# Opening stage of a two-layer diffusion trunk: squares added on the vector engine, modulation rows of five parts made between the products, three tile pairs begun instead of four

## The chip, the cores and the metric

The kernel runs as one program on one core of a Trainium2 chip. The metric is the device time of one execution in microseconds (us), as the median of repeated runs. All times inside an execution below are counted from the start of the profiled span.

## The reference

A trunk of two layers works on 256 latent tokens of 1024 features and on 256 context tokens that pass through the first layer only. Every layer is a half-step SwiGLU, a token mixer (attention with pooling in layer 0, a gated spatial unit in layer 1), and a second half-step SwiGLU. Each of the three begins with an RMS norm and a modulation whose shift, scale and gate are a product of the conditioning vector and a large matrix:

```python
def rms_norm(x, g):
    xf = x.astype(jnp.float32)
    y = xf * lax.rsqrt(jnp.mean(xf * xf, axis=-1, keepdims=True) + EPS)
    return (y * g.astype(jnp.float32)).astype(x.dtype)

def modulate(x, g, shift, scale):
    return rms_norm(x, g) * (1 + scale) + shift

def swiglu(h, w13, w2):
    a, b = jnp.split(h @ w13, 2, axis=-1)
    return (jax.nn.silu(a) * b) @ w2

# in each layer, first sub-layer:
m = (silu(c) @ w_mod[i] + b_mod[i]).reshape(b, 1, 9, d)     # the context has its own, from c_ctx
x = x + 0.5 * m[:, :, 2] * swiglu(modulate(x, norm_g[i, 0], m[:, :, 0], m[:, :, 1]), w13, w2)
```

Everything is float32. Features are 1024 = 8 parts of 128, the inner width of a SwiGLU is 2816 = 22 parts of 128.

## The kernel before

Activations lie with features on the 128 partitions, so an activation is 8 parts (index `k`) of 128 x 512: columns 0 to 255 are the latent tokens (`st` 0), 256 to 511 the context tokens (`st` 1). `X` holds the stream, `rb` the reciprocal norms of all tokens, repeated on every partition.

A float32 product is made as three products in the faster format fp32r (`mm3`): a matrix is split into a high part, which ScalarE rounds (`S.copy`, a CAST in the profile), and a low part, the remainder, which VectorE subtracts. `AH` and `AL` are the two parts of the normed activation, `sh`, `sl`, `whi` and `wlo` those of weights. One tile pair `f` of the first SwiGLU (128 columns of `a` and the 128 of `b` that belong to them) takes, for each part `k`, two groups of three products of 128 x 512.

The modulation is made in two ways. `use_mod` lets VectorE multiply 128 rows of the transposed matrix (a tile `wm`, 512 KB) with the repeated conditioning vector `cc` and sum along the row; it is needed for shift and scale of a part and for both token kinds, so four of these instructions per part. `by_rows` lets TensorE multiply the conditioning vectors (128 x 2 as the stationary operand) with natural columns of the matrix, which gives a row that is then turned to partitions by further small products. `finish_mod` adds the bias and makes `gs`, the norm's gain times (1 + scale). The two vectors `gs` and `mod` of a part are needed before its activation can be normed.

`start` is the opening stage, in which nothing can be multiplied before the norms and the first modulation are there. It

- loads the conditioning vectors, `ident`, the first `wm`, and `X` in four transfers of 512 KB, and repeats the conditioning vectors with 16 products (L630), copied by ScalarE into `cc`;
- squares the parts of `X` on ScalarE (L644), lets TensorE sum each over the partitions and over the parts in one accumulation (L645), and takes root (L646) and reciprocal (L650) of all 512 columns;
- makes the modulation of part 0 with `use_mod` and that of parts 5, 6 and 7 together in one `by_rows` (L662, L666, L669) ahead of all products;
- then goes over the parts in the order 0, 5, 1, 6, 2, 7, 3, 4, and for each makes the split of four tile pairs' weights, the normed activation, and the products of four tile pairs into 8 PSUM banks that stay open over all parts. The modulation of parts 1 to 4 is made by `use_mod` on the way.

`ffn` takes the four begun pairs over and goes on with pair 4. While it runs, `run_mods` makes the rest of the modulation at a set rate per pair.

A scheduler that records the instructions decides their order on each engine; instructions that pass through `keep_in_program_order` (`pin`) hold their order among themselves. Transfers of weights and `X` are all issued by SyncE's queue (SP), those of `run_mods` by GpSimd's (POOL). Tiles of one name share a ring of `bufs` buffers, and a transfer into a buffer waits for the last reader of it.

## Time and profile before

| | |
|---|---|
| median of 3 runs | 1154.62 us (1152.18 to 1155.01) |
| the profiled execution | 1152.68 us, its span 1150.9 us, granted TensorE clock 0.999 |
| TensorE (PE) busy | 1132.6 us, 98% of the span |
| VectorE (DVE) busy | 874.2 us, 76% |
| ScalarE (ACT) busy | 521.6 us, 45% |
| first product of the opening's tile pairs | 28.38 us |
| end of the fourth pair's last product (its Silu begins) | 73.74 us |

PE is the engine of the products, PEld its loads of stationary operands, which run beside them. A row of the timeline has the start, the duration, the engine, the line of the code, the operation, the tile written and those read, the shape, how many such instructions follow each other, and in brackets how long the engine had been idle and what ended that. A float32 product that isn't split has two records, one that is fp32r has one. Since instructions overlap in an engine's pipeline, the distance from start to start is what an instruction takes in a row of others, and the duration is how long its result takes.

### The profile page before, as it was taken

How to read it: one execution, taken by the hardware profiler on the slowest of the kernel's cores; microseconds unless marked ns; L12 is line 12 of the kernel's file. 1: busy time of each engine (PE TensorE's matmuls, PEld its weight loads, DVE VectorE, ACT ScalarE, POOL GpSimd, SP SyncE). 2: the span in 40 equal slices, each digit the busy share in tenths (PEclk: the TensorE clock that was granted, in tenths of full speed). 3: DMA queues.
4: the chain of work that ended last, by engine and by line, in shares of the span. 5: the costliest groups of instructions: out<-in, count | busy, mean ns of one | idle time of the engine just before them, and what ended most of it. 6: DMA issues, size and time to landing. Idle time of an engine off the chain costs nothing.

```text
span 1150.9 us, 19103 instructions
## 1 busy us (share of the span) xinstructions
PE 1132.6 (98%) x7646; PEld 1031.1 (90%) x7646; DVE 874.2 (76%) x1614; ACT 521.6 (45%) x814; POOL 68.4 (6%) x140
## 2 busy tenths in 40 slices
PE   8999999999999997899999999999999999999998
PEld 4878888888888895699999999999999899999998
DVE  5967787878789989778778788656767688756663
ACT  5552212222223456565334456434445866534442
POOL 0000110122222100000010000000000000000000
PEclk9999999999999999999999999999999999999999
DMA  8844656788888840556587656446546536546543
GB/s 318 309 147 156 194 185 232 275 299 317 303 289 303 318 159 10 183 183 219 180 312 261 229 193 219 162 155 225 184 142 247 185 132 210 182 152 226 179 146 116
DMA packets 52408, 242.72 MB, mean 211 GB/s; under 512 B 5600, under 2 KB 11488, under 8 KB 38880
## 3 DMA queue, kind: packets, MB, share of 16 engines
q1 hardware_dynamic: 33888, 174.39, 42.8%
q0 software_dynamic: 18432, 67.12, 17.5%
q8 instruction: 60, 0.98, 0.3%
q14 instruction: 28, 0.23, 0.1%
HBM read 240.44 MB, written 1.05 MB: 210 GB/s over the span
## 4 chain that ended last, share of the span: by engine, by line
PE 93%; DVE 4%; ACT 1%; DMA 1%; issue 1%; SPq 0%; ACTq 0%; DVEq 0%
PE ps L148 29%; PE ps L149 29%; PE ps L150 29%; PE ps L662 1%; PE ps L583 1%; PE ps L584 1%; PE ps L582 1%; PE ps L645 1%; DMA raw<-in_w 1%; PE ps L630 1%; DVE st L445 1%; DVE wlo L154 1%; DVE wm L80 1%; DVE junk L80 0%; PE ps L472 0%
## 5 line engine op out<-in xcount | busy, mean ns | idle before, releaser
L148 PE MATMUL ps<-AH,wlo 128*128 128x258 f32 (+2 forms) x1664 | 507.9, 306 | 0.3 <-ACT AH L153 0.3
L149 PE MATMUL ps<-AH,whi 128*128 128x258 f32 (+2 forms) x1664 | 507.2, 305 | 0.0
L150 PE MATMUL ps<-AL,whi 128*128 128x258 f32 (+2 forms) x1664 | 506.1, 305 | 0.0
L153 ACT CAST whi<-raw 128x1024 fp32r<-128x1024 f32 (+2 forms) x354 | 313.6, 921 | 364.5 <-PE ps L150 254.6
L154 DVE TENSOR_TENSOR wlo<-raw,whi 128x1024 fp32r<-128x1024 f32 (+2 forms) x354 | 367.7, 1065 | 53.6 <-ACT whi L153 52.8
L148 PEld LDWEIGHTS ps<-AH,wlo 128*128 128x128 f32 x1664 | 317.1, 191 | 16.3 <-issue 1.0
L149 PEld LDWEIGHTS ps<-AH,whi 128*128 128x128 f32 x1664 | 315.0, 189 | 14.7 <-issue 0.5
L150 PEld LDWEIGHTS ps<-AL,whi 128*128 128x128 f32 x1664 | 314.1, 189 | 14.2 <-DVE AL L154 0.2
L150 PE MATMUL ps<-HL,whi 128*128 128x256 f32 (+1 forms) x704 | 218.0, 310 | 0.0
L149 PE MATMUL ps<-HH,whi 128*128 128x256 f32 (+1 forms) x704 | 218.0, 310 | 0.0
L148 PE MATMUL ps<-HH,wlo 128*128 128x256 f32 (+1 forms) x704 | 218.0, 310 | 0.0
L80 DVE CUSTOM_DVE_ANT_0 wm<-wm,cc 128x1024 f32<-128x1024 f32 x138 | 165.0, 1221 | 6.1 <-DMA wm<-in_w_mod 5.4
L150 PEld LDWEIGHTS ps<-HL,whi 128*128 128x128 f32 x704 | 132.5, 188 | 7.8
L149 PEld LDWEIGHTS ps<-HH,whi 128*128 128x128 f32 x704 | 132.6, 188 | 7.7
L148 PEld LDWEIGHTS ps<-HH,wlo 128*128 128x128 f32 x704 | 132.5, 188 | 7.7
L72 POOL DMA_DIRECT2D wm<-in_w_mod x128 | 67.7, 529 | 553.8 <-DVE mod L80 507.0
L206 ACT ACTIVATE sa<-sa,cb 128x256 f32<-128x256 f32 x66 | 33.6, 510 | 120.4 <-DVE sa L205 117.0
L246 DVE SCALAR_TENSOR_TENSOR X<-ps,gate,X 128x256 f32<-128x256 f32 x64 | 30.9, 483 | 47.4 <-PE ps L150 47.2
L204 DVE COPY cb<-ps 128x1 f32<-128x1 f32 x66 | 10.3, 156 | 73.6 <-PE ps L150 73.5
L80 DVE CUSTOM_DVE_ANT_0 junk<-wm,cc 128x1024 bf16<-128x1024 f32 x34 | 41.5, 1219 | 8.8 <-ACT cc L632 8.1
L212 DVE TENSOR_TENSOR h<-ps,sa 128x512 f32<-128x512 f32 x22 | 15.2, 693 | 42.1 <-PE ps L150 33.6
L154 DVE TENSOR_TENSOR HL<-h,HH 128x256 fp32r<-128x256 f32 (+1 forms) x88 | 42.4, 485 | 0.0
(160 smaller groups left out, 709.5 us busy)
## 6 DMA issues: line engine op xcount, KB each, us to landing
raw<-in_w SPq DMA_DIRECT2D x84, 1024.0 KB, 4.9
wm<-in_w_mod POOLq DMA_DIRECT2D x128, 512.0 KB, 5.0
raw<-in_w SPq DMA_DIRECT2D x64, 704.0 KB, 4.1
wm<-in_w_mod SPq DMA_DIRECT2D x10, 512.0 KB, 6.9
raw<-in_w_in_a SPq DMA_DIRECT2D x5, 1024.0 KB, 8.5
raw<-in_w SPq DMA_DIRECT2D x8, 512.0 KB, 6.2
raw<-in_w_out_a SPq DMA_DIRECT2D x4, 1024.0 KB, 4.8
raw<-in_w_in_cu SPq DMA_DIRECT2D x4, 1024.0 KB, 4.9
```

Of the source, the lines that this page charges most:

```text
L72: eng.dma_start(out=w, in_=I["w_mod"][layer, i])
L80: pin(V.tensor_tensor_reduce(out=res, in0=w, in1=cc[:, st, :], scale=1.0, scalar=0.0, op0=ALU.mult, op1=ALU.add, accum_out=mod[:, 2 * laye ...
L148: PE.matmul(ps, wl, xh, start=first, stop=False)
L149: PE.matmul(ps, wh, xh, start=False, stop=False)
L150: PE.matmul(ps, wh, xl, start=False, stop=last)
L153: S.copy(hi, src)
L154: pin(V.tensor_tensor(out=lo, in0=src, in1=hi.bitcast(F32), op=ALU.subtract))
L206: S.activation(out=sa[:, :T], in_=sa[:, :T], func=AF.Silu, bias=cb[:, 0:1])
L212: V.tensor_tensor(out=h32[:, :n], in0=ps[1][:, :n], in1=sa[:, :n], op=ALU.mult)
L246: V.scalar_tensor_tensor(out=X[:, m, :T], in0=ps[:, :T], scalar=gate[:, 2 * layer, sub, m:m + 1], in1=X[:, m, :T], op0=ALU.mult, op1=ALU.add)
L445: V.reduce_max(out=st[:, 0:1], in_=ps[g], axis=AX.X)
L582: PE.matmul(ps[b], AL[:, k, ts], hi[:, ws], start=(k == 0), stop=False)
```

## The change

Only the opening stage is different, with the packing of its inputs.

- ScalarE squares the parts, VectorE adds them up in `acc`, and TensorE sums over the partitions once, in two halves of 256 columns. Root and reciprocal are taken in halves, too.
- `X` comes in eight transfers ahead of all weights.
- Parts 3 to 7 get their modulation from `by_rows`, one part at a time: 1 MB of natural columns, eight products of 32 columns (the vectors and zeros) by 256, put on four column groups of TensorE's array (`rw[32 * g:32 * g + 32]`) in two rounds, a copy on ScalarE, and two small products with a 0/1 matrix `sel` that add the four groups and turn the row. For each but the first part this stands between the products of the part ahead of it. Parts 0, 1 and 2 get theirs from `use_mod`.
- The order of the parts is 3, 4, 0, 5, 1, 6, 2, 7. The first part's products go in halves of 256 columns, high parts first.
- Three tile pairs are begun; the fourth is made by `ffn` like the rest.

The diff without the packing and the details of the split:

```diff
     def start():
-        ng = 4
-        order = (0, 5, 1, 6, 2, 7, 3, 4)
+        ng = 3
+        order = (3, 4, 0, 5, 1, 6, 2, 7)
+
+        jobs = {1: 0, 2: 1, 4: 2}
...
-            wm = {(0, 0): load_mod(0, 0, nc.sync)}
-            for k in range(0, NK, 2):
-                nc.sync.dma_start(out=X[:, k:k + 2], in_=I["xc"][:, k:k + 2])
-            wm[0, 1] = load_mod(0, 1, nc.sync)
...
+            for k in range(NK):
+                nc.sync.dma_start(out=X[:, k], in_=I["xc"][:, k])
+            nc.sync.dma_start(out=par, in_=I["par"])
+            rows, raws, wm = {}, {}, {}
+            rows[3] = get_rows(3)
+            raws[3] = get_raw(3)
+            rows[4] = get_rows(4)
+            raws[4] = get_raw(4)
+            wm.update({(0, j): load_mod(0, j, nc.sync) for j in range(2)})
+            raws[0] = get_raw(0)
...
             for k in range(NK):
-                sq = tmp.tile([P, 2 * T], F32, name="sq", bufs=2)
-                S.activation(out=sq, in_=X[:, k], func=AF.Square)
-                PE.matmul(ps, ones, sq, start=k == 0, stop=k == NK - 1)
-            S.activation(out=rb, in_=ps, func=AF.Sqrt, scale=1.0 / D, bias=epsb)
-            for h in range(2):
-                use_mod(0, h, wm[0, h])
-            finish_mod(0, 0, 2, slice(0, 1))
-            V.reciprocal(rb, rb)
+                square_acc(k, 2 * T)
+            ps = bank()
+            for st in range(2):
+                ts = slice(st * T, st * T + T)
+                PE.matmul(ps[:, ts], ones, acc[:, ts], start=True, stop=True)
+                S.activation(out=rb[:, ts], in_=ps[:, ts], func=AF.Sqrt, scale=1.0 / D, bias=epsb)
+            rw = bank()
+            pin(V.reciprocal(rb[:, :T], rb[:, :T]))
+
+            def by_rows(k):
+                w = rows.pop(k)
+                for kt in range(NK):
+                    g = kt % 4
+                    pin(PE.matmul(rw[32 * g:32 * g + 32, :2 * P], c32[:, kt], w[:, kt],
+                                  start=kt < 4, stop=kt >= 4))
+                row = sp.tile([P, 2 * P], F32, name="row", bufs=2)
+                pin(S.copy(row, rw[:, :2 * P]))
+                for j in range(2):
+                    PE.matmul(rw[:, 2 * P + 2 * j:2 * P + 2 * j + 2], row[:, j * P:j * P + P], sel,
+                              start=True, stop=True)
+                finish_mod(0, 0, 2, slice(k, k + 1),
+                           rw[:, 2 * P:2 * P + 4].rearrange("p (j s) -> p s j", j=2).unsqueeze(3))
...
+                if i in jobs:
+                    d = jobs[i]
                     for j in range(2):
-                        use_mod(0, 2 * nxt + j, wm.get((nxt, j)) or
-                                load_mod(0, 2 * nxt + j, nc.sync), tc.keep_in_program_order)
+                        use_mod(0, 2 * d + j, wm.pop((d, j)), tc.keep_in_program_order)
+                    finish_mod(0, 0, 2, slice(d, d + 1))
...
+                ahead = order[i + 1] if i + 1 < NK and order[i + 1] in ROWS else None
+                if i == 0:
+                    for ts in halves:
+                        if ts.start:
+                            by_rows(ahead)
+                        for j, (a, x) in enumerate(((0, AH), (0, AL), (1, AH))):
+                            for f, ab in ws:
+
+                                PE.matmul(pss[f][ab][:, ts], ws[f, ab][a], x[:, k, ts],
+                                          start=j == 0 and ts.start == 0, stop=False)
+                else:
+                    for f, ab in ws:
+                        if ahead is not None and (f, ab) == (1, 0):
+                            by_rows(ahead)
+                        mm3(pss[f][ab], *ws[f, ab], AH[:, k, :2 * T], AL[:, k, :2 * T], False,
+                            i == NK - 1)
```

What that does to the order of instructions is shown at three places. The first is VectorE's start, from the first modulation to the first normed part; in the kernel before it reads (L80 is `use_mod` and the read of its sum, L92 and L98 are `finish_mod`, L686 is the activation times `rb`):

```order
L80 ISA junk,mod<-wm,cc 128x1024
L80 ISA mod 128x1
L80 ISA wm,mod<-wm,cc 128x1024
L80 ISA mod 128x1
L80 ISA junk,mod<-wm,cc 128x1024
L80 ISA mod 128x1
L80 ISA wm,mod<-wm,cc 128x1024
L80 ISA mod 128x1
L92 TENSOR_TENSOR mod<-mod,par 128x2x2
L98 SCALAR_TENSOR_TENSOR gs<-mod,par 128x2
L650 RECIPROCAL rb<-rb 128x512
L686 TENSOR_TENSOR sa<-X,rb 128x512 x3
```

The same place on VectorE in the changed kernel (L93 and L100 are `finish_mod`, here of part 3; L714 and L726 the activation times `rb`, L696 the low parts of the weights, L704 the activation's):

```order
L638 MEMSET c_111 128x256
L165 TENSOR_TENSOR acc<-acc,sq 128x512 x7
L660 RECIPROCAL rb<-rb 128x256
L93 TENSOR_TENSOR mod<-ps,par 128x2x2
L100 SCALAR_TENSOR_TENSOR gs<-mod,par 128x2
L714 TENSOR_TENSOR sa<-X,rb 128x256
L711 RECIPROCAL rb<-rb 128x256
L696 TENSOR_TENSOR sl<-raw_99,sh 128x512
L696 TENSOR_TENSOR wlo<-raw_99,whi 128x256
L704 TENSOR_TENSOR AL<-h_190,AH 128x256
L714 TENSOR_TENSOR sa<-X,rb 128x256
L726 TENSOR_TENSOR sa<-X,rb 128x512
```

The four modulation instructions of part 0 are gone from this place, and seven additions stand there. The second place is where they went: VectorE behind the low part of part 4's activation (`h_259`); `raw_109` holds the weights of part 0, `raw_271` those of part 5.

```order
L156 TENSOR_TENSOR AL<-h_259,AH 128x512
L81 ISA junk,mod<-wm,cc 128x1024
L81 ISA mod 128x1
L696 TENSOR_TENSOR wlo<-raw_109,whi 128x256
L81 ISA wm,mod<-wm,cc 128x1024
L81 ISA mod 128x1
L81 ISA junk,mod<-wm,cc 128x1024
L81 ISA mod 128x1
L696 TENSOR_TENSOR sl<-raw_271,sh 128x512
L81 ISA wm,mod<-wm,cc 128x1024
L81 ISA mod 128x1
L696 TENSOR_TENSOR wlo<-raw_271,whi 128x256
```

The two instructions of `finish_mod` for part 0 follow it directly. The third place is TensorE from the sums of squares to the first products; before:

```order
L645 MATMUL ps<-sq,ones 128x512 x8
L662 MATMUL ps<-raw,cT 2x384 x8
L662 MATMUL ps<-whi,cT 2x384 x4
L662 MATMUL ps<-wlo,cT 2x384 x4
L669 MATMUL ps<-ident,row 128x2 x3
L148 MATMUL ps<-AH,sl 128x512
L149 MATMUL ps<-AH,sh 128x512
L150 MATMUL ps<-AL,sh 128x512
L669 MATMUL ps<-ident,row 128x2 x3
L148 MATMUL ps<-AH,sl 128x512
```

and in the changed kernel (L655 the sums, L668 and L673 a `by_rows`, first of part 3, then of part 4; L760 the products of part 3):

```order
L655 MATMUL ps<-acc,ones 128x256 x2
L668 MATMUL ps<-raw,c_111 32x256 x8
L673 MATMUL ps<-cs,row 128x2 x2
L760 MATMUL ps<-AH,sh 128x256 x4
L760 MATMUL ps<-AH,whi 128x256 x2
L760 MATMUL ps<-AL,sh 128x256 x4
L760 MATMUL ps<-AL,whi 128x256 x2
L760 MATMUL ps<-AH,sl 128x256 x4
L760 MATMUL ps<-AH,wlo 128x256 x2
L668 MATMUL ps<-raw,c_111 32x256 x8
L760 MATMUL ps<-AH,sh 128x256 x4
L673 MATMUL ps<-cs,row 128x2 x2
```

The 24 products of squares and rows ahead of the first tile pair became ten shorter ones, and the rows of the other parts stand between the products.

More of the change, by code (lines that the diff above doesn't have):

```diff
@@ L625, in start @@
-            for st in range(2):
-                for h in range(2):
-                    ps = bank()
-                    for k4 in range(4):
-                        k = 4 * h + k4
-                        PE.matmul(ps[:, k4 * P:k4 * P + P], cT[:, st, k:k + 1].broadcast_to([P, P]),
-                                  ident, start=True, stop=True)
-                    S.copy(cc[:, st, h * 512:h * 512 + 512], ps)
-            nc.sync.dma_start(out=par, in_=I["par"])
-            wn = [wpool.tile([P, 2, 2 * NR * P], F32, name=n, bufs=3 if i > 1 else 2)
-                  for i, n in enumerate(("raw", "raw", "whi", "wlo"))]
@@ L697, in start @@
[L697 to L707 removed]
+                parts = ((sh[:, k], sl[:, k], raw[:, :2]), (wh[:, k], wl[:, k], raw[:, 2]))
```

141 lines of the change are left out of this document (82 added, 59 removed).

## The prediction

> **What bounds the kernel now.** I read the page's busy times and its chain first, then the waits of PE, then windows over the opening, then the timeline there.
>
> ```profile
> PE 1132.6 (98%) x7646; PEld 1031.1 (90%) x7646; DVE 874.2 (76%) x1614; ACT 521.6 (45%) x814; POOL 68.4 (6%) x140
> PE 93%; DVE 4%; ACT 1%; DMA 1%; issue 1%; SPq 0%; ACTq 0%; DVEq 0%
> ```
>
> ```profile
> PE ps L463 <- DVE sa L451: 6.5, 5, 1.9
> PE ps L630 <- DMA ident<-in_ident: 3.3, 1, 3.3
> ...
> PE ps L148 <- ACT AH L153: 0.3, 1, 0.3
> ```
>
> TensorE bounds the kernel: once products run they wait 0.3 us in the opening and else only in the mixer (L463), which the change doesn't touch. So only the moment counts at which a given amount of tile-pair work is done. In the windows (PE, PEld, DVE, ACT busy) and PE's timeline of the opening:
>
> ```profile
> 0.00:28.38 28.38, 25.11 (x87) 12.37 (x87) 15.12 (x24) 14.79 (x26) 0.20 (x4) 1.00 0.85 317
> 28.38:75.00 46.62, 46.56 (x203) 37.35 (x203) 39.38 (x81) 26.93 (x52) 2.24 (x4) 1.00 0.68 239
> 40.00:50.00 10.00, 10.00 (x45) 8.12 (x44) 10.00 (x23) 7.38 (x15) 0.66 (x1) 1.00 0.96 336
> ```
>
> ```profile
> 3.27 6.76 PE L630 MATMUL ps<-ident,cT 128*128 128x128 f32 x32 [3.27 <-DMA ident<-in_ident]
> 9.86 7.42 PE L645 MATMUL ps<-sq,ones 128*128 128x512 f32 x16
> 17.21 5.32 PE L662 MATMUL ps<-raw,cT 128*2 128x384 f32 x16
> 22.37 2.74 PE L662 MATMUL ps<-whi,cT 128*2 128x384 f32 x8
> 24.95 2.74 PE L662 MATMUL ps<-wlo,cT 128*2 128x384 f32 x8
> 28.38 0.50 PE L148 MATMUL ps<-AH,sl 128*128 128x512 f32 x1
> ...
> 44.00 0.39 PE L148 MATMUL ps<-AH,wlo 128*128 128x512 f32 x1
> 49.56 0.40 PE L148 MATMUL ps<-AH,wlo 128*128 128x512 f32 x1
> ```
>
> ```profile
> 73.74 0.60 ACT L211 ACTIVATE sa<-ps 128x512 f32<-128x512 f32 x1 [0.27 <-PE ps L150]
> ```
>
> PE's first 28 us go to repeating (L630), squares (L645) and rows (L662). Then it is dense: 24 products from 44.00 to 49.56, 0.232 each. VectorE is full beside it (10.00 of 10) but isn't waited for: a part of the activation has 24 products, 5.6 us, and that covers what VectorE does for a later part. The 192 products of the four pairs are done at 73.7 (the Silu of pair 3 waits for the last). That is the mark: when does the changed kernel have the same four pairs (three begun, one in `ffn`)?
>
> **The change part by part.** Durations in a row, start to start, on VectorE:
>
> ```profile
> 37.76 1.22 DVE L80 CUSTOM_DVE_ANT_0 wm<-wm,cc 128x1024 f32<-128x1024 f32 x1
> ...
> 38.91 1.23 DVE L80 CUSTOM_DVE_ANT_0 junk<-wm,cc 128x1024 bf16<-128x1024 f32 x1
> ...
> 40.05 0.69 DVE L154 TENSOR_TENSOR sl<-raw,sh 128x512 fp32r<-128x512 f32 x1
> 40.66 1.22 DVE L80 CUSTOM_DVE_ANT_0 wm<-wm,cc 128x1024 f32<-128x1024 f32 x1
> ...
> 41.80 0.42 DVE L154 TENSOR_TENSOR wlo<-raw,whi 128x256 fp32r<-128x256 f32 x1
> 42.14 0.16 DVE L92 TENSOR_TENSOR mod<-mod,par 128x4 f32<-128x4 f32 x1
> ```
>
> A modulation instruction costs 1.15, a 512-wide operation 0.60, a 256-wide one 0.34. On ScalarE and for the norm:
>
> ```profile
> 2.58 1.28 ACT L623 ACT_TABLE_LOAD   x1
> 7.50 1.15 ACT L644 ACTIVATE sq<-X 128x512 f32<-128x512 f32 x2 [1.56 <-DMA X<-in_xc]
> 8.55 1.05 ACT L632 COPY cc<-ps 128x512 f32<-128x512 f32 x2
> 17.32 0.69 ACT L646 ACTIVATE rb<-ps,epsb 128x512 f32<-128x512 f32 x1 [1.22 <-PE ps L645]
> 22.15 1.09 ACT L689 ACTIVATE h<-sa,mod,gs 128x256 f32<-128x256 f32 x2 [4.15 <-DVE sa L686]
> 23.28 0.62 ACT L153 CAST AH<-h 128x512 fp32r<-128x512 f32 x1
> 27.09 0.47 ACT L666 COPY row<-ps 2x384 f32<-2x384 f32 x1 [2.06 <-PE ps L662]
> ```
>
> ```profile
> 18.04 3.35 DVE L650 RECIPROCAL rb<-rb 128x512 f32<-128x512 f32 x1 [2.53 <-ACT rb L646]
> ```
>
> ```profile
> 5.00:10.00 5.00, 5.00 (x27) 5.00 (x27) 0.85 (x1) 2.69 (x5) 0.00 (x0) 1.00 1.02 398
> ```
>
> *Squares.* `X`'s first pair landed at 7.50 with 1.12 MB moved; now its last part is at 2.17 MB, so 7.5 + 1.05 / 0.40 = 10.1, its first at 5.6. ScalarE then does a square (0.53), a table load (1.28) and root (0.3), seven squares and four copies (0.5 each), so the last square ends at 13.0, not the transfer but ScalarE last. Addition 0.69, half a sum on PE 0.6, half a root 0.46: VectorE begins the reciprocal at 15.0 instead of 18.04.
>
> *Rows.* 256 columns by L662's pace (384 columns: 5.32 - 0.49 over 15 steps, 0.32) would be 0.215 a record, two records a product. With output on two halves of the array the trace has:
>
> ```profile
> 453.24 0.63 PE L463 MATMUL ps<-ident,h 128*128 128x128 f32 x4 [0.23 <-DVE h L451]
> 453.80 1.95 PE L472 MATMUL ps<-pt,VV 128*64 128x256 f32 x16
> 455.68 0.70 PE L425 MATMUL ps<-pd,poolw 128*128 128x256 f32 x2
> ```
>
> ```profile
> 520.00:540.00 20.00, 20.00 (x168) 20.00 (x167) 16.27 (x32) 10.65 (x15) 0.53 (x1) 1.00 0.68 237
> ```
>
> At L472 the step is (1.95 - 0.38) / 15 = 0.105, half of 0.215, so halves overlap. Four groups are bounded by 0.054 (a quarter) and 0.215 (no overlap); I take 0.065, near the quarter: 16 records 1.0 us a part, plus two turning products 0.5. A block in the middle of products costs PE 1.5, and up to 0.4 more for entering and leaving (0.31 lie between the last L472 start and 455.68, against 0.105 in a row).
>
> *First part.* Rows of part 3 lie beside the reciprocal. Reciprocal half 1.7, `mod` and `gs` 0.7 with the wait for the turn, multiplication 0.4, norm on ScalarE 0.6: first product at 18.6, 9.8 earlier than 28.38. That is the whole gain. It needs no transfer later than part 3's rows (3.3 MB, 13.0).
>
> *What comes late next.* VectorE goes on in order: second reciprocal 1.7, low parts 0.6 + 0.34, `AL` 0.4, and PE's second and third group of six and the rows of part 4 (1.0), copy (0.4), turn (0.6) follow it: `gs` of part 4 at 25.1. Meanwhile PE waits 1.6 for the first `AL` and ends part 3 at 26.4. Behind `gs`, ScalarE norms part 4 (1.1), casts a weight that stands ahead (0.5) and then `AH` (0.6): part 4 starts at 27.6, after 1.2 of waiting, and ends at 31.8.
>
> From 25.1 VectorE has hardly a gap, and its order (second place shown above) puts four modulation instructions ahead of each of the next two parts that PE needs. To `gs` of part 0: five 512-wide operations (3.0), three 256-wide (1.0), four L80 (4.6), small ones (0.5), so 34.4. ScalarE norms (1.1), casts a weight (0.5) and `AH` (0.6), with hand-overs of some 0.05: PE starts part 0 at 36.9, a wait of 5.1.
>
> To `gs` of part 5: VectorE waits 1.2 until the norm of part 0 frees a buffer of `sa`; then four 512-wide (2.4), two 256-wide (0.7), four L80 (4.6), small ones (0.5): 43.9. ScalarE does three half norms (1.6) and the cast (0.6): PE starts part 5 at 46.3. Part 0, with its block of rows, took PE until 43.0, a wait of 3.3.
>
> So a part now has 18 products, 4.2 us, where VectorE needs 4.6 us for its L80 alone. Part 0's four lay between 9 and 15 us, where VectorE was free (15.12 of 28.38); now they stand in its full stretch, and what PE won by starting early it waits away at parts 0 and 5.
>
> *The rest.* After 46.3 PE has five parts of 18 and pair 3's 48 products, 138 x 0.232 = 32.0, two more rows blocks (3.1), about 1.0 before part 6 (its turn leaves nine products, 2.1, to cover `gs`, norm and cast, 3.0), and 0.2 of small hand-overs: 82.6. Before: 73.7. Sum +8.9. Check on PE alone: 18.6 + 192 products 44.5 + four blocks 6.2 + waits 13.3 = 82.6.
>
> *Edits at nothing.* The seven additions (4.2) lie in VectorE's free time beside ScalarE's squares; without that cover they would cost their 4.2. The fourth pair's move into `ffn` is the same products. Its weights wait on SP for the buffer of part 6's rows, which PE reads near 52; 1 MB at 0.40 takes 2.6 and lands by 58, its first use is after 67. Part 3's halves are two products of 256 for one of 512: the window just quoted, in a stage with 256 latent tokens, has 168 records in 20 us, 0.12 each, so 0.3 in all. On SP the rows of part 5 wait for PE to have read part 3's (16), with part 5's weights and part 1's `wm` behind them; these land between 23 and 27 and are used from 28 on. If a transfer came late there, its lateness would add to a wait of part 0 that is there anyhow. `run_mods` gets one more turn, beside 11 us of products. POOL's queue starts as before.
>
> Against the profiled execution 1152.68 + 8.9 = 1161.6. It lies 1.9 under the median 1154.62, so by the median 1163.5; I put 1162.5, between the two. About 0.3%, 3.5 us, is what a measurement here can tell from no change.
>
> **The rivals.**
>
> *A, TensorE runs at half pace in the gaps' wake.* L630's 32 records of 128 x 128 take 6.76, 0.21 each, while L463's four of the same shape are begun within 0.56 (453.24 to 453.80), 0.14 each. The slow ones follow 3.27 us of idleness, though the granted clock reads 1.00 in both. Now PE idles from 10.0 to 13.8 and for 5 us before part 0; the trace of before has no wait over 1.9 once PE has begun. If all PE work from the sums to part 4 went at half pace, the half sum (+0.4), two blocks of rows with their turns (+3.0) and the groups of six ahead of part 4's rows (+2.2) would lie on the path: 5.6 to 5.8, so 1168. Were part 0 alone slow, its 4.2 would grow into the wait of part 5 and push part 5's rows by 2: 1164.5. The Trainium skill, "TensorE: Matmul & The Clock Gate", Part 1, "What's actually happening", says the array's clock falls to half after an idle window of about 3.4 us and rises after a busy one of that length. By that rule the gap at 10.0 is just long enough and the sum would be 1168 instead of 1162.5; the trace agrees for the start (0.21 against 0.14) and has no such gap to show the rest. Chance 0.22.
>
> *B, the column groups don't overlap.* A block of rows takes 16 x 0.215 = 3.4 instead of 1.0. On top of the forecast the first two lie on the path to `gs` of part 4 (+4.8), part 5's fills a wait, and parts 6's and 7's stand between products (+5): 1172. For it speaks that no row shows four groups, against it L472 with two. Chance 0.07.
>
> *C, the change gains: PE sets the pace.* Were VectorE's stretch from `gs` of part 4 to `gs` of part 5 not waited for, PE would be done at 18.6 + 44.5 + 6.2 = 69.3, 4.4 us earlier than 73.7: 1149. It decides where `gs` of part 5 comes before 35.0 (43.9 less 8.9). VectorE's rows in that stretch add to 18 us without a wait, so even a start 3 us earlier isn't enough. Chance 0.07.
>
> *D, no change to tell.* The gap is half closed if the path to `gs` of part 4 is VectorE's own work alone (two half reciprocals 3.4, three 512-wide and three to four 256-wide 3.1, small ones 0.8, so 7.5 to 7.9 instead of 10.1: -2.2), the rows go at the quarter pace (-0.7) and part 6 finds its `AH` ready (-1.0): 78.7, +5, and +4 with `X` a microsecond sooner: 1157 to 1158. Chance 0.09.
>
> **How the numbers follow.** The forecast has 0.55, with its own range from 1158.5 (the tight path to part 4) to 1167 (rows at the two-group pace of 0.105 with 0.4 for switching: each block 1.1 longer, two of them on the path and two more behind 46.3, +4.2). Faster: C, 0.07. Same: D, 0.09. Slower: the forecast, A and B, 0.84. The range leaves out B above and C and half of D below: 1156.5 to 1169.
>
> **What would show it.** First product near 18.6; rows blocks of about 1 us; PE waiting for `AH` of part 0 some 5 us with L80 rows on VectorE until then, for part 5 some 3; pair 3's Silu near 82.6. Wrong, if PE has no wait over 2 us between 25 and 47, or `gs` of part 5 stands before 35.

## The result, and the profile after

The changed kernel takes 1168.11 us (median, 1165.49 to 1170.34), the kernel before beside it 1153.55; the ratio is 1.0125, with a 95% interval of 1.0094 to 1.0156. It is slower, by 14.6 us where 8 to 9 were forecast. The profiled execution took 1165.49 us, its span 1163.7, that is 12.8 more than the span before.

For a comparison at equal work I use the Silu of the fifth tile pair's first half, which in both kernels comes after the same 216 products of the opening and of `ffn`. It stands in ScalarE's timeline, before and after:

```profile
79.99 0.60 ACT L211 ACTIVATE sa<-ps 128x512 f32<-128x512 f32 x1 [0.83 <-PE ps L150]
```

```profile
92.75 0.60 ACT L213 ACTIVATE sa<-ps 128x512 f32<-128x512 f32 x1 [3.10 <-PE ps L152]
```

The distance is 12.76 us, as much as the spans differ by: the whole loss lies ahead of this mark, and nothing is lost or won behind it in this execution. The busy times on the page and TensorE's waits (total, times, longest) answer to the two views that the prediction began with:

```profile
PE 1130.0 (97%) x7708; PEld 1032.6 (89%) x7708; DVE 870.8 (75%) x1605; ACT 521.8 (45%) x813; POOL 68.4 (6%) x140
```

```profile
PE ps L150 <- ACT AH L155: 8.7, 5, 4.8
...
PE ps L647 <- ACT c L639: 4.1, 1, 4.1
PE ps L655 <- DVE acc L165: 3.2, 1, 3.2
...
PE ps L760 <- ACT AH L700: 1.5, 1, 1.5
```

TensorE is 2.6 us less busy in a span that is 12.8 longer. It now waits 8.7 us for `AH`, 8.4 of them in the opening, besides a wait of 3.2 for the added squares that wasn't there. (The 0.3 that the page of before has for `AH` isn't in the opening, as the prediction took it: over the first 95 us TensorE has no such wait there. Nothing in the forecast hangs on it.) Its timeline, in the order of time:

```profile
13.83 1.22 PE L655 MATMUL ps<-acc,ones 128*128 128x256 f32 x2 [3.17 <-DVE acc L165]
15.62 1.22 PE L655 MATMUL ps<-acc,ones 128*128 128x256 f32 x2 [0.56 <-ACT rb L656]
16.77 1.94 PE L668 MATMUL ps<-raw,c 128*32 128x256 f32 x16
19.20 1.01 PE L673 MATMUL ps<-cs,row 128*128 128x2 f32 x4 [0.49 <-ACT row L671]
21.69 1.22 PE L760 MATMUL ps<-AH,sh 128*128 128x256 f32 x4 [1.48 <-ACT AH L700]
...
26.79 1.10 PE L668 MATMUL ps<-raw,c 128*32 128x256 f32 x16
...
31.68 0.50 PE L150 MATMUL ps<-AH,sl 128*128 128x512 f32 x1 [0.92 <-ACT AH L155]
...
40.87 0.80 PE L150 MATMUL ps<-AH,sl 128*128 128x512 f32 x1 [4.76 <-ACT AH L155]
...
50.08 0.50 PE L150 MATMUL ps<-AH,sl 128*128 128x512 f32 x1 [1.75 <-ACT AH L155]
```

The first product stands at 21.69 instead of 28.38. The four starts at 21.69 (part 3), 31.68 (part 4), 40.87 (part 0) and 50.08 (part 5) are 10.0, 9.2 and 9.2 apart, where 18 products take 4.2. Two identical blocks of rows are in the list: 16 records take 1.94 us at 16.77 and 1.10 at 26.79. The windows show the difference (window and its length, then busy PE, PEld, DVE, ACT and POOL, each with its count of instructions, then the granted clock, DMA share, GB/s):

```profile
10.00:15.00 5.00, 1.83 (x8) 0.97 (x7) 3.31 (x5) 3.48 (x7) 0.00 (x0) 0.82 1.02 403
15.00:20.00 5.00, 3.94 (x23) 1.90 (x22) 1.75 (x1) 2.14 (x5) 0.00 (x0) 0.50 1.01 393
20.00:25.00 5.00, 2.93 (x13) 2.55 (x13) 4.47 (x9) 1.85 (x4) 0.00 (x0) 0.50 0.76 290
...
40.00:45.00 5.00, 4.13 (x23) 2.26 (x24) 5.00 (x9) 1.96 (x6) 0.35 (x1) 0.66 0.45 160
```

TensorE was granted half its clock from about 13 to 27 us and again for about 3.4 us behind the wait of 4.76; below, *half pace* is this state. VectorE's timeline between the scales (`gs`, L100) of parts 4, 0 and 5:

```profile
29.30 0.16 DVE L100 SCALAR_TENSOR_TENSOR gs<-mod,par 128x2 f32<-128x2 f32 x1
...
32.44 1.22 DVE L81 CUSTOM_DVE_ANT_0 junk<-wm,cc 128x1024 bf16<-128x1024 f32 x1
...
38.50 0.16 DVE L100 SCALAR_TENSOR_TENSOR gs<-mod,par 128x2 f32<-128x2 f32 x1
...
41.63 1.22 DVE L81 CUSTOM_DVE_ANT_0 junk<-wm,cc 128x1024 bf16<-128x1024 f32 x1
...
47.68 0.23 DVE L100 SCALAR_TENSOR_TENSOR gs<-mod,par 128x2 f32<-128x2 f32 x2
```

9.2 us lie between each two, with four modulation instructions (L81 now) in each stretch, and TensorE's starts follow them at the same distance.

So there were two theories to try. *Theory 1*: TensorE's half pace in the wake of its waits makes the loss bigger than forecast. *Theory 2*: the modulation instructions on VectorE, now between the scales, make the loss that was forecast. Besides, each of the change's parts could be tried alone.

### The profile page after: what moved, and what is told of

The parts are those of the page before. It is cut to its first block, busy times and chain, and to the rows that moved or that the text cites. A ratio compares the mean times of both kernels' runs of the same rounds, so it can differ in the third digit from the quotient of the medians.

```text
span 1163.7 us, 19232 instructions
## 1 busy us (share of the span) xinstructions
PE 1130.0 (97%) x7708; PEld 1032.6 (89%) x7708; DVE 870.8 (75%) x1605; ACT 521.8 (45%) x813; POOL 68.4 (6%) x140
## 4 chain that ended last, share of the span: by engine, by line
PE 92%; DVE 4%; ACT 1%; DMA 1%; issue 1%; SPq 0%; DVEq 0%; ACTq 0%
PE ps L150 29%; PE ps L151 29%; PE ps L152 29%; DMA raw<-in_w 1%; PE ps L585 1%; PE ps L586 1%; PE ps L584 1%; DVE st L447 1%; DMA X<-in_xc 1%; PE ps L474 1%; DVE junk L81 0%; DVE wm L81 0%; PE ps L668 0%; PE ps L760 0%; ACT h L700 0%
## 5 line engine op out<-in xcount | busy, mean ns | idle before, releaser
L155 ACT CAST whi<-raw 128x1024 fp32r<-128x1024 f32 (+1 forms) x340 | 310.1, 946 | 374.0 <-PE ps L152 272.3
L156 DVE TENSOR_TENSOR wlo<-raw,whi 128x1024 fp32r<-128x1024 f32 (+1 forms) x340 | 363.7, 1095 | 60.9 <-ACT whi L155 59.8
L81 DVE CUSTOM_DVE_ANT_0 wm<-wm,cc 128x1024 f32<-128x1024 f32 x134 | 159.8, 1218 | 5.0 <-DMA wm<-in_w_mod 4.4
L155 ACT CAST HH<-h 128x256 fp32r<-128x256 f32 (+1 forms) x88 | 39.7, 455 | 0.8 <-DVE h L210 0.8
```

The costliest lines, as they stand in the source:

```text
L81: pin(V.tensor_tensor_reduce(out=res, in0=w, in1=cc[:, st, :], scale=1.0, scalar=0.0, op0=ALU.mult, op1=ALU.add, accum_out=mod[:, 2 * laye ...
L155: S.copy(hi, src)
L156: pin(V.tensor_tensor(out=lo, in0=src, in1=hi.bitcast(F32), op=ALU.subtract))
```

## The experiments

The kernels' first products, the mark (that Silu of the fifth pair), its distance from the kernel before (79.99), and the times; first product and mark are of one profiled execution, and times are medians with the 95% interval of the ratio to the kernel before:

| kernel | first product | mark | to before | us | ratio |
|---|---|---|---|---|---|
| before | 28.38 | 79.99 | | 1152.8 to 1153.6 | |
| changed | 21.69 | 92.75 | +12.8 | 1168.11 | 1.0094 to 1.0156 |
| e1_warm | 20.74 | 90.86 | +10.9 | 1163.62 | 1.0075 to 1.0126 |
| e2_nomod | 20.60 | 84.79 | +4.8 | 1157.67 | 1.0026 to 1.0054 |
| e6_nomod_warm | 21.51 | 83.95 | +4.0 | 1159.33 | 1.0041 to 1.0078 |
| e8_early | 22.93 | 86.70 | +6.7 | 1161.97 | 1.0063 to 1.0091 |
| e3_squares | 32.56 | 83.81 | +3.8 | 1157.95 | 1.0027 to 1.0058 |
| e12_squares_warm | 31.99 | 83.41 | +3.4 | 1157.56 | 1.0021 to 1.0044 |
| e4_rows | 27.19 | 80.17 | +0.2 | 1154.55 | 1.0002 to 1.0020 |
| e5_rows_warm | 30.82 | 81.41 | +1.4 | 1156.16 | 1.0019 to 1.0042 |
| e10_fit | 26.70 | 77.38 | -2.6 | 1150.77 | 0.9969 to 0.9995 |
| e9_three | 27.68 | 85.05 | +5.1 | 1160.82 | 1.0038 to 1.0073 |
| e7_pairs | 25.56 | 77.36 | -2.6 | 1151.64 | 0.9976 to 0.9996 |
| e11_both | 30.23 | 80.82 | +0.8 | 1152.98 | 0.9982 to 1.0004 |

A mark carries about a microsecond of chance: the repeating of the vectors, the same 32 records in each, takes 5.3 to 6.8 us in these executions (6.76 in the kernel before), and where TensorE goes on from it without a wait all that follows is moved.

**e1_warm: filler products in TensorE's waits.** Products whose result nobody reads, behind the repeating, behind part 3's turn and ahead of part 0:

```diff
+            def fill(n):
+                for _ in range(n):
+                    pin(PE.matmul(rw, ident, X[:, 0], start=True, stop=True))
+            fill(7)
             for k in range(NK):
                 square_acc(k, 2 * T)
```

> The changed kernel, with products that nobody reads put where TensorE stood idle: seven of 128 x 512 float32 between the repeating of the vectors and the sums, two behind part 3's turn, nine ahead of part 0. Everything else is as it was. Theory 1 (the gaps put TensorE at half pace, and that is what the forecast's walk lacked): rows of part 3 take 1.1 us instead of 1.94, part 0's first six products 1.4 instead of 2.9, the first product begins near 19.6 instead of 21.69, the fourth pair is done some 3.5 to 4.5 us earlier, and the time is 1161 to 1164. Rival (the extra over the walk is waits between engines, and the slow records are only a sign of them): the products run no faster where it counts, time within 1.5 us of the changed kernel or above it by the fillers.

1163.62 us, 4.5 under the changed kernel. No window of the opening shows a clock below 1.00, and the stretch that went at 0.50 reads:

```profile
15.00:20.00 5.00, 3.94 (x28) 1.91 (x27) 2.36 (x5) 2.14 (x5) 0.00 (x0) 1.00 1.02 397
```

Half pace is thus shown to cost, but 1.9 us at the mark of the profiled execution and not the 3.5 to 4.5 that I expected; 10.9 of the 12.8 remain. The medians lie 4.5 apart, from four executions each: three of e1_warm at 1163.2 to 1163.7 and one at 1169.1, those of the changed kernel at 1165.5, 1166.2, 1170.0 and 1170.3 with mean clocks of 0.991, 0.988, 0.987 and 0.987. The intervals of the ratios overlap, and where the slower ones lost their time no trace shows.

The 1.9 is a lower bound, since the fillers hold the kernel back, too (L663 the sums, L655 the fillers):

```profile
15.31 0.59 PE L663 MATMUL ps<-acc,ones 128*128 128x256 f32 x2
...
34.24 7.89 PE L655 MATMUL ps<-X,ident 128*128 128x512 f32 x18
41.56 0.80 PE L150 MATMUL ps<-AH,sl 128*128 128x512 f32 x1
```

The sums begin at 15.31 instead of 13.83, and part 0 begins at 41.56, though the cast of its `AH` had ended at 39.1. Between those places half pace can be priced: from the first sum to the first product 7.9 us in the changed kernel and 5.4 here, and from there to the scale of part 4 7.6 and 6.8, so 3.2 us in all up to that scale.

**e2_nomod: the changed kernel without the twelve modulation instructions.**

```diff
-        jobs = {1: 0, 2: 1, 4: 2}
+        jobs = {}
+        V.memset(mod, 0.25)
+        V.memset(gs, 1.0)
```

> The changed kernel without the twelve L81 instructions on VectorE for parts 0, 1 and 2 (their modulation is left at constants, so that part of the computation is left out). Theory 2 (the waits at parts 0 and 5 are VectorE's modulation work in its full stretch): no wait over 1.5 us at either, the first product stays at 21.7, part 4 starts at 31.7, and from there PE needs 174 products, 40.4, three blocks 4.6 and 2 to 3 us of short waits: done at 79 to 80 instead of 87.1, time 1157 to 1160, still slower than before. Rival (casts, norms and transfers hold part 0 as well): waits of 3 us or more stay, time above 1163.

1157.67 us; 8.0 of the 12.8 at the mark are gone, although the clock in its windows between 15 and 30 us is still 0.65 to 0.68. TensorE's waits for `AH` shrink from 8.7 us to 2.4:

```profile
PE ps L150 <- ACT AH L155: 2.4, 4, 0.9
```

Theory 2 holds, and it carries the larger part. The kernel is still slower than before.

**e6_nomod_warm: both repairs.** e2_nomod with e1_warm's fillers, but for those ahead of part 0:

```diff
-        jobs = {1: 0, 2: 1, 4: 2}
+        jobs = {}
...
+            fill(7)
             for k in range(NK):
                 square_acc(k, 2 * T)
...
-            by_rows(order[0])
+            by_rows(order[0], 2)     # two fillers behind the turn
```

> The changed kernel without the twelve modulation products of parts 0 to 2 on VectorE (those constants are left out of the computation) and with filler products in TensorE's idle stretches of the opening. If the two causes, the moved modulation on VectorE and the half pace on TensorE, are apart and add, their prices of about 10.5 (e2_nomod) and 4.5 us (e1_warm) come off together: 1152 to 1155, ratio 1.000 to 1.002, about the kernel before. Rival (both are parts of one wait and overlap, so that taking away the second brings little): 1156 to 1158, ratio 1.003 to 1.005.

1159.33 us, not better than e2_nomod's and above even the rival's 1158. I expected the prices to add; here they don't. The clock is 1.00 in every window of the opening, and yet 4.0 us stay at the mark (4.8 without the fillers). It isn't a clean sum, though, since the seven fillers are too long again:

```profile
16.08 0.59 PE L665 MATMUL ps<-acc,ones 128*128 128x256 f32 x2
```

The sums begin at 16.08 where e2_nomod has 13.68, and the first product at 21.51 instead of 20.60. Whether the prices would add with fillers that fit wasn't tried. What the changed kernel still loses with both causes gone begins with its waits:

```profile
PE ps L150 <- ACT AH L155: 2.5, 3, 1.4
PE ps L772 <- DVE AL L716: 1.2, 1, 1.2
PE ps L665 <- ACT rb L666: 0.6, 1, 0.6
PE ps L681 <- ACT row L679: 0.5, 1, 0.5
```

These are 4.8 us of small waits behind the sum. From the first product to the mark TensorE takes 62.4 us, against 51.6 in the kernel before. Of the 10.8 between them the first two of these waits make 3.7, and about 6 are the four blocks of rows that now stand between the products, 1.5 each: where one stands, two products begin 1.33 us apart instead of 0.23, and around its turn 0.60.

**e8_early: part 0's four instructions at another place.** They stand right behind the first half of the reciprocal, where VectorE waits for the turned row, and not between part 4's and part 0's scales:

```diff
-        jobs = {1: 0, 2: 1, 4: 2}
+        jobs = {2: 1, 4: 2}
...
             pin(V.reciprocal(rb[:, :T], rb[:, :T]))
+            for j in range(2):
+                use_mod(0, j, wm.pop((0, j)), pin)
+            finish_mod(0, 0, 2, slice(0, 1))
```

> The changed kernel with part 0's modulation on VectorE placed right behind the first half of the reciprocal, in the stretch in which VectorE waits, instead of between the modulation of parts 4 and 5. Nothing of the computation is left out. If the place of those four products and not their number is what makes TensorE wait at parts 0 and 5, the waits of 4.8 and 1.8 us there shrink to under 1.5 each and the time is 5 to 8 us under the changed kernel's: 1160 to 1163, ratio 1.006 to 1.009. Rival (VectorE is the bound of the whole opening, so a moved product is paid elsewhere): under 2 us gained, 1166 to 1169.

1161.97 us, 6.1 under the changed kernel in both the time and the mark, as expected: the same instructions at another place. TensorE's wait of 4.8 at part 0 is gone, and in the first 95 us none for the `AH` of a part behind the first is over 0.9:

```profile
PE ps L150 <- ACT AH L155: 2.5, 3, 0.9
```

Moving four instructions brings three quarters of what leaving out twelve does, though the first product comes 1.2 us later (22.93). (Their two `wm` loads go ahead of part 3's rows, and the copies into `cc` ahead of the sums, which begin no later for it: 13.66.)

**e3_squares: the squares' step alone, in the kernel before.**

```diff
             for k in range(NK):
-                sq = tmp.tile([P, 2 * T], F32, name="sq", bufs=2)
-                S.activation(out=sq, in_=X[:, k], func=AF.Square)
-                PE.matmul(ps, ones, sq, start=k == 0, stop=k == NK - 1)
+                square_acc(k, 2 * T)
+            ps = bank()
+            PE.matmul(ps, ones, acc, start=True, stop=True)
```

> The kernel before with one part of the change: squares added on VectorE and summed once on TensorE; all else as before. If the squares' 7.4 us on TensorE were what delays the products: the rows begin at 11 to 13 instead of 17.2 and the time falls by 4 to 6 us. By the order VectorE gets, where the last addition stands behind the fourth L80 of part 0 (which waits for a transfer that landed at 12.6): the sum comes at 16.5 to 17.5 as before, and since TensorE is idle from 10 to 16 it runs the rows at half pace, 16 to 20 us instead of 10.8: slower by 2 to 6 us.

1157.95 us. In TensorE's timeline the sum comes no earlier than the end of the eight sums before (17.28), since in VectorE's order the modulation of part 0 stands between the additions, and sum and rows go at half pace behind the wait:

```profile
17.33 2.07 PE L644 MATMUL ps<-acc,ones 128*128 128x512 f32 x2 [8.69 <-DVE acc L163]
19.33 7.38 PE L661 MATMUL ps<-raw,cT 128*2 128x384 f32 x16
```

The same 16 records took 5.32 before.

**e12_squares_warm: the same with seven fillers in that wait.**

```diff
+            for _ in range(7):
+                pin(PE.matmul(fb, ident, X[:, 0], start=True, stop=True))
             for k in range(NK):
                 square_acc(k, 2 * T)
```

> e3_squares (the kernel before, squares added on VectorE) with seven filler products in TensorE's wait for that sum, 8.7 us long in e3_squares. It splits the price of the squares' step. Theory (4.2 us of a later first product, of which about 2 are the rows' first block and the sum at half pace and 2 are the reciprocal that comes 2.1 us later): rows' first block 5.3 us instead of 7.4, first product at about 30 instead of 32.6, time 1155 to 1156.5, ratio 1.0015 to 1.003. Rival (VectorE's order alone makes the price): as e3_squares, 1157.5 to 1158.5.

1157.56 us: 0.4 at the mark, not the 2 that I gave to half pace, and a time in the rival's range. The fillers ended 2.08 us ahead of the sum, and that was enough for the clock to fall once more:

```profile
18.12 1.85 PE L648 MATMUL ps<-acc,ones 128*128 128x512 f32 x2 [2.08 <-DVE acc L163]
19.90 6.25 PE L665 MATMUL ps<-raw,cT 128*2 128x384 f32 x16
```

The rows got back half of their loss (6.25 against 7.38), but TensorE also began 1.1 us later in this execution, which the mark contains. So this run doesn't tell the two apart: the price of the squares' step is 3.4 to 3.8 us here, with its split between VectorE's order and the clock left open.

**e4_rows: the tiled rows alone, in the kernel before.** Parts 5 to 7 still together and ahead of all products, on four column groups:

```diff
-                        PE.matmul(ps[j][0:2, :NR * P], cT[:, :, k],
+                        g = 32 * (k % 4)
+                        PE.matmul(ps[j][g:g + 32, :NR * P], c32[:, k],
                                   wn[k // 2][:, k % 2, j * NR * P:(j + 1) * NR * P],
-                                  start=k == 0, stop=k == NK - 1)
+                                  start=k < 4, stop=k >= 4)
```

> The kernel before with another part of the change: the rows of parts 5, 6 and 7 in products of 32 columns on four column groups, from the same transfers and at the same place. Four groups at 0.08 a record of 384 columns: 32 records 2.6 us instead of 10.8, but their last quarter lands at 20.4, so they end near 21.5 instead of 27.6, and the first product waits for the split of the weights instead, near 25.2 instead of 28.4. Time 1149 to 1152, 2.5 to 4 us faster. If the groups did not overlap: no change.

1154.55 us, no gain and a miss, though the rows end at 21.3 instead of 27.6. Then TensorE waits, and the first products go at half pace:

```profile
24.27 1.50 PE L675 MATMUL ps<-sel,row 128*128 128x2 f32 x12 [2.97 <-ACT row L672]
...
27.19 0.77 PE L148 MATMUL ps<-AH,sl 128*128 128x512 f32 x1 [1.43 <-DVE sl L154]
27.76 0.63 PE L149 MATMUL ps<-AH,sh 128*128 128x512 f32 x1
```

They are 0.43 apart up to 32.9, against 0.23.

**e5_rows_warm and e10_fit: fillers in those two waits.** First six behind the rows and three behind the turn, then three and one:

```diff
                     pin(PE.matmul(ps[j][g:g + 32, :NR * P], c32[:, k],
...
+                fill(3)          # six in e5_rows_warm
...
                     pin(PE.matmul(ps[:, 2 * i:2 * i + 2], row[:, i * P:i * P + P], sel,
                                   start=True, stop=True))
+                fill(1)          # three in e5_rows_warm
```

> The kernel before with the column-tiled rows of parts 5 to 7 (as e4_rows) and filler products behind the rows and behind the turn, so that TensorE has no long idle stretch ahead of the first products. Nothing of the computation is left out. Theory 1 (half pace after an idle stretch ate the gain of the quicker rows): the products behind the turn run at 0.23 us instead of 0.43, no window from 20 to 35 us shows a clock below 0.9, and the time is 151 under e4's by 2 to 4 us against e4_rows, so 1150.5 to 1152.5, ratio 0.998 to 1.000. Rival (the rows never bound anything, ScalarE and VectorE set the first products): same as e4_rows, 1154 to 1155.

A miss: 1156.16 us. The clock stayed at 1.00, but I had made the fillers too long: a filler takes 0.9 us, and the twelve records behind the rows ended at 27.4, three us after the copy of the rows was there, so the first product came at 30.82.

> e5_rows_warm with half the filler products: three behind the rows (2.7 us, as long as the wait there was in e4_rows) and one behind the turn, so that they end when the first operand is ready and not 3 us after. Theory 1 (half pace ate what the quicker rows gave): first product at 27 to 27.7 us at 0.23 us each, against 28.4 before; the time 1151.5 to 1153, ratio 0.998 to 1.000. Rival (the rows' gain is bounded by the arrival of their data and by ScalarE's copies in any case): first product not before 28.4, time 1153 to 1155.

With fillers as long as the waits:

```profile
22.23 2.84 PE L677 MATMUL ps<-X,ident 128*128 128x512 f32 x6
24.91 1.40 PE L684 MATMUL ps<-sel,row 128*128 128x2 f32 x12
26.16 1.10 PE L677 MATMUL ps<-X,ident 128*128 128x512 f32 x2
26.70 0.80 PE L148 MATMUL ps<-AH,sl 128*128 128x512 f32 x1
```

The first product is earlier than in e4_rows by 0.5 us, the mark by 2.8, and the time, 1150.77, beats both kernels (ratio to before 0.9982, 0.9969 to 0.9995). Half pace had eaten the gain of the tiled rows. That is shown, since the two kernels differ in nothing but the fillers and the pinned order of the rows, and with the same pinned order e5_rows_warm lost.

**e9_three: three pairs instead of four, alone, in the kernel before.**

```diff
-        ng = 4
+        ng = 3
...
-                split(wh[1][:, k], wl[1][:, k], raw[:, 3])
```

> The kernel before with three tile pairs in the opening instead of four; all else (squares, rows, modulation on VectorE) as before, and the fourth pair's 48 products follow as one piece. Nothing of the computation is left out. Theory (four pairs give VectorE's modulation its cover: 24 products, 5.6 us, to each part; with 18, 4.2 us, TensorE must wait for VectorE): VectorE's last scale comes at about 57 us, part 4 starts at about 60, and with 18 + 48 products behind it the same work ends at about 75.5 to 77 instead of 74.1: 1154.5 to 1156.5, ratio 1.0015 to 1.003. Rival (the number of pairs costs nothing by itself): 1152.5 to 1153.5.

1160.82 us, well beyond my 1154.5 to 1156.5: +5.1 at the mark, and 3.0 more behind it in the profiled execution, which has three stretches of half pace in the mixer where that of the kernel before has one. In the opening TensorE now waits 3.3 us for `AH`, 2.28 of it ahead of the last part, and in the wake of that wait goes at half pace:

```profile
58.09 0.50 PE L148 MATMUL ps<-AH,sl 128*128 128x512 f32 x1 [2.28 <-ACT AH L153]
...
59.15 0.63 PE L148 MATMUL ps<-AH,sl 128*128 128x512 f32 x1
59.57 0.63 PE L149 MATMUL ps<-AH,sh 128*128 128x512 f32 x1
```

From the first product to the mark it takes 57.4 us instead of 51.6. Waits of 3.3 and a stretch of half pace, 3.4 us long and so worth 1.7, make 5.0 of these 5.8; at the mark 5.1 show, since the first product came 0.7 earlier by the chance named above. In mechanism the theory held (18 products don't cover what VectorE does for a part), and its size was too small because I had left out half pace once more.

**e7_pairs: squares added by twos.** The kernel before with four additions on VectorE and four sums on TensorE instead of eight:

```diff
+            for k in range(0, NK, 2):
+                sq = [tmp.tile([P, 2 * T], F32, name=n, bufs=2) for n in ("sq", "h32")]
+                for i in range(2):
+                    S.activation(out=sq[i], in_=X[:, k + i], func=AF.Square)
+                V.tensor_tensor(out=sq[0], in0=sq[0], in1=sq[1], op=ALU.add)
+                PE.matmul(ps, ones, sq[0], start=k == 0, stop=k == NK - 2)
```

> The kernel before with the squares of two tiles added on VectorE and only four instead of eight summing products on TensorE; the order of all else as before. If the tail of the sum on TensorE sets the start of the reciprocal, the sum ends at about 15.5 instead of 17.3 us and the first product moves up by 1 to 2.5 us: 1150.5 to 1152, ratio 0.998 to 0.999. Rival (the adds hold VectorE's order back as in e3_squares, the reciprocal comes no earlier): same or slower, 1153 to 1156.

1151.64 us, 0.9986 (0.9976 to 0.9996): faster than before. From the repeating on TensorE never waits longer than 0.9 us in the opening, and the rows begin at 14.39 instead of 17.21:

```profile
14.39 5.32 PE L664 MATMUL ps<-raw,cT 128*2 128x384 f32 x16
```

The first product stands at 25.56. About 1 of these 2.8 us is chance (the sums of the kernel before follow the repeating without a wait, and it ended at 9.86 there and at 8.83 here), and the medians differ by 1.6. This is the squares' step with its benefit, and without the wait.

**e11_both: e7_pairs with e10_fit's rows and fillers.**

> e10_fit and e7_pairs together: squares of two tiles added on VectorE, rows of parts 5 to 7 column-tiled, and the four fillers. If the two edits each move up their own end of the same chain (the sum 2.8 us earlier, the rows 1 us), the first product starts at 24 to 25.5 us and the time is 1149.5 to 1151.5, ratio 0.997 to 0.9985. Rival (the rows wait for their data until 20 us and VectorE is full from 30 us on, so that nothing comes on top of e7_pairs): 1151.5 to 1153.

1152.98 us, same as before. The rival has the number; the trace has a reason that neither had named. With sums and rows both short, TensorE runs ahead of the transfers and waits for each, about 1 us at a time, and behind those waits the clock is halved:

```profile
19.06 0.90 PE L672 MATMUL ps<-whi,c 128*32 128x384 f32 x4 [1.05 <-DMA whi<-in_w_modr]
21.03 0.85 PE L672 MATMUL ps<-wlo,c 128*32 128x384 f32 x2 [1.07 <-DMA wlo<-in_w_modr]
```

```profile
20.00:25.00 5.00, 3.97 (x20) 0.96 (x20) 2.55 (x5) 2.19 (x4) 0.00 (x0) 0.50 0.99 362
```

This is one execution, of 1154.91 us. Four of the twelve took 1150.5 to 1151.4 at mean clocks of 0.997 to 0.998; whether their clock was halved there, too, no trace shows.

## Why the prediction was right or wrong

The sign, the mechanism and the range were right: 1168.1 lies in 1156.5 to 1169.0, near its upper end. The size was 5.6 us short of the median, and that the median meets rival A's 1168 is in part luck, as the steps show. By its own steps, in the profiled execution:

*The mark.* The Silu at 73.74 waits for the first half of pair 3; the second half's three products end at 74.3. So 0.6 of the forecast loss wasn't one: 82.6 less 74.3 would have been +8.3.

*Squares.* VectorE began the reciprocal at 15.60 (forecast 15.0): the half sum took 1.22 instead of 0.6, since it went at half pace (0.59 in e1_warm). What was overlooked is the second half sum: it writes the bank that the first root still reads, so it waited 0.56 for it, at half pace again, and the rows, which stand behind it in TensorE's order, began at 16.77 instead of 15.0.

*Rows.* At full clock, a block of 16 records takes 1.10, in steps of about 0.05 (1.10 less the 0.38 of a last record, over 15): the four column groups overlap fully, 1.0 was right, and rival B fell. The first block took 1.94 and its turn 1.01 instead of 0.6.

*First part.* First product 21.69, forecast 18.6. The 3.1 are the three delays above: 1.8 until the rows begin, 0.8 in the block, 0.4 in the turn. The forecast had the rows beside the reciprocal; here VectorE, done with its first half, waited 2.95 for their turn.

*What comes late next.* The scale of part 4 came at 29.30, 7.6 after the first product where 6.5 was forecast; the groups of six went at half pace. From there on the forecast holds: 9.2 and 9.2 us from scale to scale (9.3 and 9.5 forecast); part 4 to part 0 to part 5 9.2 and 9.2 apart (9.3 and 9.4). The wait at part 0 is 4.8 (5.1 forecast). The one at part 5 is 1.8 instead of 3.3, since part 0's products and rows went at half pace into it and VectorE set the start all the same. e2_nomod and e8_early confirm this step from the other side: at the mark 8.0 us come back without the instructions, and 6.1 if only part 0's four stand elsewhere.

*The rest.* From the start of part 5 to the end of the fourth pair 37.0 us, 36.3 forecast.

The sum, from 82.6: 3.1 + 1.1 - 0.4 + 0.7 gives 87.1, where the trace has that end (the cast at 87.13 waits for it). The step that failed is the choice between the forecast and rival A. A had said that TensorE's work from the sums to part 4 would go at half pace, worth 5.6 to 5.8, and had come to 1168; I gave it 0.22. It happened, but not for as long as A had it: half pace ended at about 26.9 us, ahead of the second block of rows, which took 1.10. So of the 4.5 us that the fourth pair's end lies over the forecast, half pace makes 3.2 by the comparison with e1_warm, 2.4 ahead of the first product and 0.8 from there to the scale of part 4. The second half sum's wait for its bank makes 0.6, and the rest is small and wasn't tried. The profiled execution is 3.9 over the forecast (1165.49 against 1161.6); the others are up to 8.7 over it at lower mean clocks, and where they lost the rest isn't shown.

The evidence against A was read too narrowly: "the trace of before has no wait over 1.9 once PE has begun" is true, but half pace is in that trace, in the mixer, as a window of before has it:

```profile
430.00:440.00 10.00, 7.71 (x41) 6.12 (x41) 8.58 (x27) 8.05 (x15) 0.14 (x2) 0.83 0.03 8
```

The Trainium skill, "TensorE: Matmul & The Clock Gate", Part 1, "What's actually happening", speaks of an idle window of about 3.4 us. The direction agrees: behind waits of 3.17 and 4.76 the clock was half. Read as a threshold for one wait, it is too lenient here: waits of 2.28 us in e9_three and 2.08 in e12_squares_warm, and in e11_both a row of waits of about 1.0, were followed by half pace.

Rivals C and D had no part in it: VectorE's stretch was waited for as forecast, and the path to part 4 was longer, not tighter.

*What the parts are worth.* At the mark of the kernel before the squares alone cost 3.8 us, the tiled rows 0.2, three pairs instead of four 5.1. These don't divide the 12.8: in e3_squares it is part 0's modulation between the additions that delays the sum, and the changed kernel has none there; its first product comes 6.7 us earlier than before. The prediction had put all of the loss on the modulation's new place and on 18 products instead of 24 to a part, with squares and rows as gains, and the fourth pair's move into `ffn` "at nothing". In the kernel before, the fourth pair was the cover: the same VectorE work beside 18 products already makes TensorE wait. The changed kernel with four pairs, the order of the parts and the halves of the first part weren't tried by themselves.

## What to carry to other kernels

Before work is taken off the bounding engine, see what the engine will do in the freed time: where it can only wait for the next operand, shorter work brings nothing, and the pace after the wait may take back more than was won; filling the hole with products that nobody reads, no longer than the hole, turned a useless edit into a gain of 2.7 us here. A side engine that is full but never waited for has its cover from the products beside it: count products per step against that engine's work per step before fewer of them are made. And try the parts of an edit alone: two of the three here had a form that gains by itself (sums by twos, tiled rows with a fitted filler; together they gained nothing), while the whole lost 14.6.

## What the hardware showed beside

Half pace comes in pieces. In e4_rows and e9_three the products go at 0.43 for stretches whose ends can be read off: 59.15 to 62.5 in e9_three is 3.4 us. In the changed kernel's windows half pace adds up to 13.7 us between 10 and 30 us, four times 3.4, and to 3.4 behind the wait of 4.76. Ten-us windows of the mixer read 1.00 or 0.83 in the kernel before and in e7_pairs, and 0.83 is 3.4 us at half in ten. One such piece takes 1.7 us of TensorE's time, 0.0015 of the mean clock over this span. The profiled executions of this case have one to three of them in the mixer, where TensorE is busy for 7.4 to 8.6 of 10 us in the rows shown. That of the kernel before had one there (the row above); that of e7_pairs had three, in the windows

```profile
430.00:440.00 10.00, 7.42 (x38) 5.73 (x38) 8.45 (x28) 5.92 (x11) 0.28 (x4) 0.83 0.06 15
...
450.00:460.00 10.00, 8.60 (x48) 4.82 (x46) 8.12 (x23) 6.56 (x15) 0.00 (x0) 0.83 0.00 0
460.00:470.00 10.00, 7.96 (x47) 4.77 (x48) 7.70 (x20) 5.82 (x16) 0.69 (x2) 0.83 0.30 105
```

and so gave back, 350 us later, all of the 2.6 us that it had won in the opening (still 2.6 ahead at 444 us, 0.6 behind at 480): its profiled span is 1151.5 against 1150.9, while its median is lower by 1.6. That executions of one kernel differ by the same draw is likely by their mean clocks, though not shown: the kernel before took 1151.5 us in an execution at 0.999, mostly 1152.2 to 1153.8 at 0.997 and 1155.3 to 1155.7 at 0.995 (four at 0.997 took 1154.5 to 1155.2, so the mean clock isn't all); e10_fit 1150.0 at 0.999 and 1154.3 at 0.995. A gain of 2 us in such a kernel is seen only at equal clocks or over many executions, and what sets the draw in the mixer stayed open.

Four column groups of 32 columns overlap fully: 16 records of 256 columns begin 0.05 apart, against 0.215 (by the pace of the rows before) for one that takes the array alone.
